# Two couples of heads weighed directly behind each other, into the two halves of one PSUM bank, with five buffers of turned weights

## The chip, the cores and the metric

The kernel runs on one core of a Trainium2 chip. The metric is the device time of one execution in microseconds (us), the median of several runs. A core has five engines that work through their own queues in order: TensorE (PE in the profile, its weight loads PEld), VectorE (DVE), ScalarE (ACT), GpSimd (POOL) and SyncE (SP, which here only issues DMAs). They wait for each other through semaphores.

## The reference

A trunk of two decoder layers over 256 positions of width 2048, in float32. Every layer is `x <- LN(alpha*x + mixer(x))` and then `x <- LN(alpha*x + sqrelu_mlp(x))`. The mixer of layer 0 has sliding-window attention A (16 query heads, 2 key heads, sinks) and dilated attention B (8 heads, three patterns that are merged by their softmax denominators). The mixer of layer 1 has stick-breaking attention C (16 heads, no softmax) and latent attention D (16 heads). The part that the change touches is, in each of them, the last line of this:

```
s = einsum('bqhd,bshd->bhqs', q, k) * scale      # scores
p = softmax(where(valid, s + bias, -inf))        # or the stick-breaking weights
o = einsum('bhqs,bshd->bqhd', p, v)              # the values are weighed
y = concat(heads of both groups);  out = einsum('bse,ed->bsd', y, w_out)
```

## The kernel before, in words

All weights come from memory as units of 128 x 1024 float32. `Stream._split` makes a high part (`w_hi`, ScalarE, L120) and a low part (`w_lo`, VectorE, L121) of each, and every projection is three products: high by high, low by high, high by low. `ws` (L329, L332) writes features to partitions, `as_` (L379 to L381) positions. Both work unit by unit, and between two units they call `pump`, which does one step of attention (`attn_step`). So attention is woven into the projections: the projections keep TensorE busy while ScalarE and VectorE work on the weights of attention.

Attention runs in jobs: A (16 heads), B0 and B1 (4 heads with 3 patterns each), C0, D0, C1, D1 (8 heads each). A step takes a couple of heads, and on TensorE writes its scores (`qk`, L708, tiles `sc`). VectorE and ScalarE then make weights `S` of them in the following steps. A flip (`flip`, L260) transposes the weights of one head on TensorE into the tile `pt`, and ScalarE copies that to `pT` (L262); each step does at most one flip. Two steps behind the flip of a couple's second head comes the weighing (`weigh`): four matmuls (L279 and L281) of 64 output columns of the array, the even head into partitions 0 to 63 and the odd head into 64 to 127 of the tile `o`, which has 256 columns of float32 and one buffer, a PSUM bank. The two heads' fp32 matmuls show as 4 instructions for each of the two lines. With the last pattern of a couple, `o` is evicted: ScalarE casts it to the high part of `y` (L285), and VectorE makes the low part of `o` and the high part (L286). In B1, C1 and D1 the tiles that take the place of `y` are named `x`.

Within one step the order on the queues is: the weighing, the flip, the stages of VectorE and ScalarE, then the scores of the next couple (the number behind `at_step`'s step is that order). What `pump` calls first are small functions that were put off (`late`), among them the rotation of D's queries (`rotate`, L982 to L984, on VectorE). `pT` has four buffers, `S` four.

Of the kernel before, what the change touches and what calls it, by code (L numbers as in the profile page):

```python
# [11 lines left out]
F32 = mybir.dt.float32  # L12
F32R = mybir.dt.float32r
BF16 = mybir.dt.bfloat16
# [4 lines left out]
P = 128  # L19
S = 256  # L20
# [143 lines left out]
class Trunk:  # L164
    def __init__(self, tc, ctx, args):
        self.tc = tc
        self.nc = tc.nc
        self.a = args
        self.split_ahead = 3
        self.dma_ahead = 5  # L170
        pool = lambda name, bufs, **kw: ctx.enter_context(tc.tile_pool(name=name, bufs=bufs, **kw))
        self.const = pool("const", 1)
        self.raw = pool("raw", 6)
        self.spl = pool("spl", 4)
        self.res = pool("res", 1)
        self.small = pool("small", 5)
        self.ps = pool("ps", 1, space=bass.MemoryType.PSUM)
        self.w = Stream(self)
        self.side = deque()
        self.late = deque()  # L180
        self.todo = deque()
        self.due = {}
        self.flips = deque()
        self.s_live = 0
        self.i = 0
        self.turn = 0
# [26 lines left out]
    def attn_step(self):  # L213
        i = self.i
        self.i += 1
        if self.flips and self.flips[0][0] <= i:
            _, job, h, u = self.flips.popleft()
            self.at_step(i, 2, self.flip, job, h, u)
            if h % 2:
                self.at_step(i + 2, 1, self.weigh, job, (h - 1, h), u)  # L220
        for _, _, fn, args in sorted(self.due.pop(i, []), key=lambda t: t[:2]):
            fn(*args)
        if not self.todo or i < self.turn:
            return
        job, h, u = self.todo[0]
        per, pair = job.per, (h, h + 1)
        if h not in job.s:
            need = 2 if per > 1 else 1
            if self.s_live + need > self.s_bufs:
                return  # L230
            self.s_live += need
            if per > 1:
                for g in pair:
                    job.s[g] = self.at.tile([P, per * 384], F32, name="S", bufs=self.s_bufs)
            else:
                both = self.at.tile([P, 768], F32, name="S", bufs=self.s_bufs)
                job.s[h], job.s[h + 1] = both[:, 0:384], both[:, 384:768]
        self.todo.popleft()
        self.turn = i + job.pace
        scs = [self.ps.tile([P, 384], F32, name="sc", bufs=2) for _ in pair]  # L240
        self.qk(scs, [job.score(g, u) for g in pair])
        for j, (g, sc) in enumerate(zip(pair, scs)):
            job.stages[0](g, u, sc, job.s[g])
            if u == per - 1:
                for n, fn in enumerate(job.stages[1:]):
                    self.at_step(i + j + 1 + n, 3, fn, g, job.s[g])
        if u == per - 1:
            self.flips.extend((i + j + job.lag, job, g, v) for v in range(per) for j, g in enumerate(pair))
# [5 lines left out]
    def flip(self, job, h, u):  # L254
# [9 lines left out]
        if u == job.per - 1 and (job.per > 1 or h % 2):  # L264
            self.s_live -= 1

    def weigh(self, job, heads, u):
        nc = self.nc
        first, last = u == 0, u == job.per - 1
        if first and heads[0] % 2 == 0:  # L270
            job.o = self.ps.tile([P, S], F32, name="o")
        o = job.o
        for blk in range(2):
            for h in heads:
                rows = slice((h % 2) * HD, (h % 2) * HD + HD)
                w = job.pt[(h, u)]
                v = job.value(h, u, blk)
                if blk == 0:
                    nc.tensor.matmul(o[rows, :], v, w[:, 0:S], start=first, stop=False, skip_group_check=True)  # L279
                else:  # L280
                    nc.tensor.matmul(o[rows, P:S], v, w[:, S:S + P], start=False, stop=last, skip_group_check=True)  # L281
        if last and heads[-1] % 2:
            y = job.y(len(job.out))
            yh, yl, _ = y
            nc.scalar.copy(yh, o)  # L285
            nc.vector.tensor_tensor(yl, o, yh.bitcast(F32), op=ALU.subtract)  # L286
            job.out.append(y)
            job.left -= 1
# [155 lines left out]
    def setup(self):  # L444
        nc, a, const = self.nc, self.a, self.const
        self.x = self.res.tile([P, 2, D], F32, name="x_res")
        xv = a["x"][0].rearrange("(t p) d -> p t d", p=P)
        cuts = (0, 256, 512, 1024, 1536, 2048)
        for c0, c1 in zip(cuts[:1], cuts[1:]):
            nc.scalar.dma_start(self.x[:, :, c0:c1], xv[:, :, c0:c1])  # L450
        nc.scalar.preload_act_table_set("natural_log_exp_and_others")
        zeros = self.at.tile([P, 512], BF16, name="zeros")
        nc.vector.memset(zeros, 0.0)
        self.keep_clock(IDLE[0], zeros)
        self.ident = const.tile([P, P], F32, name="ident")
        nc.sync.dma_start(self.ident, a["ident"])
        self.w._dma(1)
        for c0, c1, ahead in zip(cuts[1:], cuts[2:], (2, 4, 5, 6)):
            nc.sync.dma_start(self.x[:, :, c0:c1], xv[:, :, c0:c1])
            self.w._dma(ahead)  # L460
        gb = self.at.tile([16, 8, P], F32, name="gb")
        rg = self.at.tile([6, P], F32, name="rg")
        self.sinks = const.tile([P, 16], F32, name="sinks")
        self.masks = self.at.tile([P, 4, 384], F32, name="masks")
        small = [(gb[:, i * 2:i * 2 + 2, :], a[nm].rearrange("l (k p) -> k l p", p=P))
                 for i, nm in enumerate(("ln1_g", "ln1_b", "ln2_g", "ln2_b"))]
        small += [(rg[0:4, :], a["odd_q_norm_g"][0].rearrange("(k p) -> k p", p=P)),
                  (rg[4:6, :], a["odd_kv_norm_g"][0].rearrange("(k p) -> k p", p=P)),
                  (self.masks, a["m_even"]), (self.sinks, a["even_sinks"][0].unsqueeze(0).to_broadcast([P, 16]))]

        def load(some):
            for dst, src in some:
                nc.gpsimd.dma_start(dst, src)

        def gate():

            nc.gpsimd.tensor_copy(self.masks[:, 0, 0:1], self.xT[10][0][:, 0:1].bitcast(F32))

        self.late.extend([lambda: None] * 6)
        self.late.append(gate)  # L480
        self.late.extend(lambda some=small[i:i + 2]: load(some) for i in range(0, 8, 2))
        self.mhalf = const.tile([P, 2], F32, name="mhalf")
        nc.vector.memset(self.mhalf, -0.5)
        self.xT = LazyTiles(self.transposed(None))
        self.gbc = const.tile([P, 134], F32, name="gbc")
        self.side.append(self.gains(gb, rg))
# [380 lines left out]
    def odd(self):  # L867
        nc = self.nc
        self.masks = self.at.tile([P, 2, 384], F32, name="masks")
        self.rope_f = self.at.tile([P, S], F32, name="rope_f")  # L870
        self.rope_t = self.at.tile([P, 2, 64], F32, name="rope_t")
        for t, nm in ((self.rope_t, "rope_t"), (self.rope_f, "rope_f"), (self.masks, "m_odd")):
            self.late.append(lambda t=t, nm=nm: nc.gpsimd.dma_start(t, self.a[nm]))
        cq = self.as_(self.xT, KT, 512)
        zq = self.rms(cq, 512)
        self.pump()
        ck = self.as_(self.xT, KT, 288)
        kr = self.at.tile([P, 2, 96], F32, name="kr", bufs=1)
        nc.gpsimd.memset(kr[:, :, 0:64], 0.0)
        kt_ = self.at.tile([P, 2, 32], F32, name="krt", bufs=1)  # L880
        ks = self.at.tile([P, 2, 32], F32, name="krs", bufs=1)
        for t in range(2):
            rt = self.rope_t[:, t, :]
            nc.vector.tensor_copy(ks[:, t, 0:16], ck[t][:, 272:288])
# [255 lines left out]
    def go(self):  # L1140
        tc = self.tc
        self.plan()
        for layer in range(2):
            if layer == 0:
                self.s_bufs, self.pt_bufs, self.qk_bufs, self.y_bufs = 4, 4, {"qk": 15}, 10
            else:
                self.s_bufs, self.pt_bufs, self.qk_bufs, self.y_bufs = 4, 4, {"c": 8, "d": 10}, 14
            with tc.tile_pool(name=f"at{layer}", bufs=1) as self.at:
                if layer == 0:
                    self.setup()  # L1150
                last, st = self.even() if layer == 0 else self.odd()
                assert not self.side and not self.todo
            self.layer_norm(last, st, 1, layer)
            with tc.tile_pool(name=f"mp{layer}", bufs=1) as self.mp:
                last, st = self.mlp(layer)
                if layer == 1:
                    self.final(last, st)
            if layer == 0:
                self.layer_norm(last, st, 2, layer)
# [33 lines left out]
```

## Time and profile before

| | us |
|---|---|
| median of 3 runs | 2181.27 (2180.08 to 2182.53) |
| the profiled execution | 2179.61 |
| its span in the trace | 2177.8 |
| PE busy | 2160.6 (99%) |
| DVE busy | 1393.6 (64%) |
| ACT busy | 1064.2 (49%) |

Busy time is the union of an engine's instructions in the trace; the ends of matmuls are modelled, so for TensorE the start of one instruction to the start of the next is the better measure. A row of the timeline merges equal instructions that follow each other. In square brackets stands how long the engine was idle before the row, and what released it; "issue" is time in which it waited for nothing that the profile shows.

### The profile page before, as it was taken

What the parts mean: (1) busy time and instruction counts of PE and PEld (TensorE: products, weight loads), DVE (VectorE), ACT (ScalarE), POOL (GpSimd) and SP (SyncE); (2) the same over time, 40 slices, a digit from 0 to 9 for tenths busy, and PEclk for the clock granted to TensorE, in tenths of its full rate; (3) what the DMA queues carried; (4) which work ended last, traced back from release to release, by engine and by line L of the source; (5) the groups of instructions that cost most, each with busy time, mean ns of one, the idle gap of its engine ahead of it and who ended that gap; (6) DMA issues with size and microseconds to landing.
All of it is one profiled execution on the core that took longest, in us unless ns stands there. A gap on an engine that the chain in (4) does not pass through costs nothing.

```text
span 2177.8 us, 29447 instructions
## 1 busy us (share of the span) xinstructions
PE 2160.6 (99%) x11323; PEld 1816.3 (83%) x11324; DVE 1393.6 (64%) x1912; ACT 1064.2 (49%) x1532; POOL 35.3 (2%) x65
## 2 busy tenths in 40 slices
PE   9999999999999999999999999999999999999998
PEld 8878887888888888888888887778888888888886
DVE  5765566775465556456568888878645655554656
ACT  4554444554354345355345667545534534543542
POOL 0000000000000000000012000000000000000000
PEclk9999999999999999999999999999999999999999
DMA  8446554665656665656558544466565656556553
GB/s 278 148 134 182 157 164 148 197 197 195 192 184 199 191 190 193 193 176 202 191 151 212 170 143 149 153 196 209 202 193 175 203 194 192 184 197 190 185 200 118
DMA packets 222269, 399.02 MB, mean 183 GB/s; under 512 B 12778, under 2 KB 52416, under 8 KB 221360
## 3 DMA queue, kind: packets, MB, share of 16 engines
q1 hardware_dynamic: 219152, 386.51, 56.3%
q0 software_dynamic: 2416, 9.84, 2.0%
q8 instruction: 88, 1.44, 0.3%
q10 hardware_dynamic: 560, 0.79, 0.1%
q14 instruction: 53, 0.43, 0.1%
HBM read 395.00 MB, written 2.10 MB: 182 GB/s over the span
## 4 chain that ended last, share of the span: by engine, by line
PE 94%; issue 2%; DVE 1%; DMA 1%; ACT 1%; POOL 1%; POOLq 0%; SPq 0%; ACTq 0%; DVEq 0%
PE acc L332 18%; PE acc L379 15%; PE acc L380 15%; PE acc L381 15%; PE acc L329 9%; PE sc L332 5%; PE sc L329 3%; PE pt L332 3%; PE o L332 3%; PE sc L708 2%; PE o L329 1%; PE pt L329 1%; PE pt L260 1%; PE o L279 1%; DVE w_lo L121 1%
## 5 line engine op out<-in xcount | busy, mean ns | idle before, releaser
L121 DVE TENSOR_TENSOR w_lo<-raw,w_hi 128x1024 fp32r<-128x1024 f32 (+3 forms) x748 | 883.9, 1198 | 601.7 <-ACT w_hi L120 597.7
L120 ACT CAST w_hi<-raw 128x1024 fp32r<-128x1024 f32 (+3 forms) x748 | 760.1, 1030 | 729.7 <-PE acc L381 439.8
L332 PE MATMUL acc<-x,w_hi 128*128 128x512 f32 x1824 | 453.8, 394 | 2.7 <-DVE x L529 2.5
L379 PE MATMUL acc<-w_hi,h_hi 128*128 128x512 f32 x1016 | 395.3, 389 | 0.0
L380 PE MATMUL acc<-w_lo,h_hi 128*128 128x512 f32 x1016 | 395.3, 389 | 0.0
L381 PE MATMUL acc<-w_hi,h_lo 128*128 128x512 f32 x1016 | 395.2, 389 | 0.0
L332 PEld LDWEIGHTS acc<-x,w_hi 128*128 128x128 f32 x1824 | 331.2, 189 | 66.6 <-ACT w_hi L120 2.5
L329 PEld LDWEIGHTS acc<-x,w_lo 128*128 128x128 f32 x1824 | 243.2, 190 | 17.8 <-issue 3.8
L329 PE MATMUL acc<-x,w_lo 128*128 128x256 f32 x1824 | 253.8, 284 | 0.0
L381 PEld LDWEIGHTS acc<-w_hi,h_lo 128*128 128x128 f32 x1016 | 190.7, 188 | 39.6
L379 PEld LDWEIGHTS acc<-w_hi,h_hi 128*128 128x128 f32 x1016 | 190.8, 188 | 39.4
L380 PEld LDWEIGHTS acc<-w_lo,h_hi 128*128 128x128 f32 x1016 | 190.8, 188 | 39.2
L332 PE MATMUL sc<-x,w_hi 128*128 128x512 f32 x512 | 138.7, 392 | 0.0
L379 PE MATMUL acc<-w_hi,x 128*128 128x512 f32 (+1 forms) x304 | 119.5, 393 | 0.3 <-DVE x L528 0.2
L381 PE MATMUL acc<-w_hi,x 128*128 128x512 f32 (+1 forms) x304 | 115.8, 381 | 0.0
L380 PE MATMUL acc<-w_lo,x 128*128 128x512 f32 (+1 forms) x304 | 115.7, 381 | 0.0
L345 ACT ACTIVATE xfull<-acc 128x256 f32<-128x256 f32 x130 | 49.7, 384 | 127.7 <-PE acc L332 77.5
L332 PEld LDWEIGHTS sc<-x,w_hi 128*128 128x128 f32 x512 | 91.1, 189 | 14.6
L329 PE MATMUL sc<-x,w_lo 128*128 128x256 f32 x512 | 84.3, 282 | 0.0
L329 PEld LDWEIGHTS sc<-x,w_lo 128*128 128x128 f32 x512 | 76.6, 190 | 6.4
L332 PE MATMUL pt<-x,w_hi 128*128 128x512 f32 x256 | 79.3, 391 | 0.0
L332 PE MATMUL o<-x,w_hi 128*128 128x512 f32 x256 | 78.9, 389 | 0.0
(209 smaller groups left out, 1956.4 us busy)
## 6 DMA issues: line engine op xcount, KB each, us to landing
raw<-in_mlp_w SPq DMA_DIRECT2D x512, 512.0 KB, 3.9
raw<-in_even_w_in SPq DMA_DIRECT2D x92, 512.0 KB, 4.1
raw<-in_odd_w_in SPq DMA_DIRECT2D x56, 512.0 KB, 4.5
raw<-in_odd_w_out SPq DMA_DIRECT2D x32, 512.0 KB, 3.6
raw<-in_even_w_out SPq DMA_DIRECT2D x24, 512.0 KB, 3.9
gb_rows<-in_ln_g POOLq DMA_DIRECT2D x3, 1024.0 KB, 5.0
gb_rows<-in_ln_b POOLq DMA_DIRECT2D x3, 1024.0 KB, 7.1
raw<-in_odd_w_uq SPq DMA_DIRECT2D x8, 384.0 KB, 4.7
```

The source lines that it names most:

```text
L120: nc.scalar.copy(h, r)
L121: nc.vector.tensor_tensor(l, r, h.bitcast(F32), op=ALU.subtract)
L260: nc.tensor.transpose(pt[:, b * P:(b + 1) * P], st[:, u * 384 + b * P:u * 384 + (b + 1) * P], self.ident)
L279: nc.tensor.matmul(o[rows, :], v, w[:, 0:S], start=first, stop=False, skip_group_check=True)
L329: nc.tensor.matmul(banks[f][:, S:2 * S], lo[:, c:c + P], xs[kt + kk][0], start=False, stop=wide and kt + kk == nkt - 1, skip_group_check=True)
L332: nc.tensor.matmul(banks[f], hi[:, c:c + P], xs[kt + kk][2], start=kt + kk == 0, stop=not wide and kt + kk == nkt - 1, skip_group_check=True)
L345: nc.scalar.activation(t, bank[:, S:2 * S], AF.Copy, scale=scale)
L379: nc.tensor.matmul(outs[t], xh[:, ts], hi[:, c:c + width], start=first, stop=False, skip_group_check=True)
L380: nc.tensor.matmul(outs[t], xh[:, ts], lo[:, c:c + width], start=False, stop=False, skip_group_check=True)
L381: nc.tensor.matmul(outs[t], xl[:, ts], hi[:, c:c + width], start=False, stop=last, skip_group_check=True)
L708: nc.tensor.matmul(sc[:, cols], q[:, qs], k[:, ks], start=True, stop=True, skip_group_check=True)
```

## The change

`weigh_two` now stands where `weigh` was called. It keeps the arguments of a weighing until there are two, and then does both. The tile `o` is 512 columns wide, a whole bank, and the couples take its halves in turn. Since the turned weights of a couple are held until the next couple's are there, `pT` gets a fifth buffer. To make room for it, small tiles that are needed early (`zeros`, the gains `gb` and `rg`, the rotary table `rope_t` and three tiles of the shared rotary key) are put into buffers of `pT` and `S`.

```diff
@@ -181,6 +181,8 @@
         self.flips = deque()
+        self.pend = []
+        self.o_half = 0
         self.s_live = 0
@@ -217,7 +219,7 @@
             if h % 2:
-                self.at_step(i + 2, 1, self.weigh, job, (h - 1, h), u)
+                self.at_step(i + 2, 1, self.weigh_two, job, (h - 1, h), u)
@@ -264,11 +266,22 @@
+    def weigh_two(self, *args):
+
+        self.pend.append(args)
+        if len(self.pend) == 2:
+            for a in self.pend:
+                self.weigh(*a)
+            self.pend = []
+
     def weigh(self, job, heads, u):
         nc = self.nc
         first, last = u == 0, u == job.per - 1
-        if first and heads[0] % 2 == 0:
-            job.o = self.ps.tile([P, S], F32, name="o")
+        if first:
+            if self.o_half == 0:
+                self.o_bank = self.ps.tile([P, 2 * S], F32, name="o")
+            job.o = self.o_bank[:, self.o_half * S:(self.o_half + 1) * S]
+            self.o_half = 1 - self.o_half
         o = job.o
@@ -449,7 +462,7 @@
-        zeros = self.at.tile([P, 512], BF16, name="zeros")
+        zeros = self.at.tile([P, 512], BF16, name="pT", bufs=self.pt_bufs)
@@ -458,8 +471,8 @@
-        gb = self.at.tile([16, 8, P], F32, name="gb")
-        rg = self.at.tile([6, P], F32, name="rg")
+        gains = self.at.tile([16, 9, P], F32, name="S", bufs=self.s_bufs)
+        gb, rg = gains[:, 0:8, :], gains[0:6, 8, :]
@@ -868,17 +881,15 @@
-        self.rope_t = self.at.tile([P, 2, 64], F32, name="rope_t")
+        early = self.at.tile([P, 2, 224], F32, name="S", bufs=self.s_bufs)
+        self.rope_t, kr, kt_, ks = (early[:, :, a:b] for a, b in ((0, 64), (64, 160), (160, 192), (192, 224)))
...
-        kr = self.at.tile([P, 2, 96], F32, name="kr", bufs=1)
         nc.gpsimd.memset(kr[:, :, 0:64], 0.0)
-        kt_ = self.at.tile([P, 2, 32], F32, name="krt", bufs=1)
-        ks = self.at.tile([P, 2, 32], F32, name="krs", bufs=1)
@@ -1142,9 +1153,9 @@
-                self.s_bufs, self.pt_bufs, self.qk_bufs, self.y_bufs = 4, 4, {"qk": 15}, 10
+                self.s_bufs, self.pt_bufs, self.qk_bufs, self.y_bufs = 4, 5, {"qk": 15}, 10
             else:
-                self.s_bufs, self.pt_bufs, self.qk_bufs, self.y_bufs = 4, 4, {"c": 8, "d": 10}, 14
+                self.s_bufs, self.pt_bufs, self.qk_bufs, self.y_bufs = 4, 5, {"c": 8, "d": 10}, 14
```

What this makes of the queues is seen best in the order of the instructions. A row is the line, the operation, what it writes and reads (buffer numbers of tiles left out), the size of what it writes, and the semaphores that it waits for: DVE_49 counts what VectorE has done, Activation_49 what ScalarE has done. The lines of the changed kernel are 13 higher here (L279 is L292, L281 is L294, L286 is L299, L260 is L262).

This is TensorE's queue before, where the first couple of job A is weighed, in a step between two units of the projection (`acc`):

```order
L381 MATMUL acc<-w_hi,x_126 128x512
L279 MATMUL o<-pT,qk 64x256 x2
L281 MATMUL o<-pT,qk 64x128 x2
L260 MATMUL pt<-ident,S 128x128 [waits DVE_49,Activation_49]
L260 MATMUL pt<-ident,S 128x128 [waits DVE_49]
L260 MATMUL pt<-ident,S 128x128
L708 MATMUL sc<-qk 128x128 [waits DVE_49] x2
L708 MATMUL sc<-qk 128x256 x2
```

Two steps further on in the same queue, before, the second couple is weighed:

```order
L381 MATMUL acc<-w_hi,x_181 128x512
L279 MATMUL o<-pT,qk 64x256 [waits DVE_49]
L279 MATMUL o<-pT,qk 64x256
L281 MATMUL o<-pT,qk 64x128 x2
L260 MATMUL pt<-ident,S 128x128 [waits Activation_49]
L260 MATMUL pt<-ident,S 128x128 x2
L708 MATMUL sc<-qk 128x128 [waits DVE_49] x2
L708 MATMUL sc<-qk 128x256 x2
```

And this is TensorE's queue in the changed kernel at this second place:

```order
L394 MATMUL acc<-w_hi,x_180 128x512
L292 MATMUL o<-pT,qk 64x256 x2
L294 MATMUL o<-pT,qk 64x128 x2
L292 MATMUL o<-pT,qk 64x256 [waits DVE_49]
L292 MATMUL o<-pT,qk 64x256
L294 MATMUL o<-pT,qk 64x128 x2
L262 MATMUL pt<-ident,S 128x128 [waits Activation_49]
L262 MATMUL pt<-ident,S 128x128 x2
L721 MATMUL sc<-qk 128x128 x2
L721 MATMUL sc<-qk 128x256 x2
```

The first weighing has moved from the first place to the second, and the wait for VectorE stands between the two weighings.

VectorE's queue before, where the second couple of D0 is evicted, behind a rotation of queries (`d`, `rope_f`):

```order
L346 SCALAR_TENSOR_TENSOR d<-acc,xfull 128x256 [waits Activation_49] x4
L982 TENSOR_TENSOR rtmp<-d,rope_f 32x512 [waits DVE_49]
L983 TENSOR_TENSOR d<-d,rope_f 32x512
L984 TENSOR_TENSOR d<-d,rtmp 32x512 [waits DVE_49]
L286 TENSOR_TENSOR y<-o,y 128x256 [waits Activation_49]
```

The same place of VectorE's queue in the changed kernel:

```order
L359 SCALAR_TENSOR_TENSOR d<-acc,xfull 128x256 [waits Activation_49] x4
L993 TENSOR_TENSOR rtmp<-d,rope_f 32x512 [waits DVE_49]
L994 TENSOR_TENSOR d<-d,rope_f 32x512
L995 TENSOR_TENSOR d<-d,rtmp 32x512 [waits DVE_49]
L299 TENSOR_TENSOR y<-o,y 128x256 [waits Activation_49] x2
```

Both couples' low parts now stand behind the rotation; the second weighing on TensorE stands between them.

## Rows read from the trace of the kernel before

**Rows 1.** The page: the span, and TensorE's busy time.

```profile
span 2177.8 us, 29447 instructions
PE 2160.6 (99%) x11323; PEld 1816.3 (83%) x11324; DVE 1393.6 (64%) x1912; ACT 1064.2 (49%) x1532; POOL 35.3 (2%) x65
```

**Rows 2.** Windows: length, busy us (instructions) of PE, PEld, DVE, ACT, POOL; clock, DMA.

```profile
90.00:160.00 70.00, 70.00 (x423) 54.62 (x422) 52.47 (x132) 42.60 (x112) 0.00 (x0) 1.00 0.48 140
1235.00:1435.00 200.00, 199.72 (x1108) 160.48 (x1107) 162.27 (x310) 128.71 (x265) 0.00 (x0) 1.00 0.47 148
```

**Rows 3.** Timeline (start, us, engine, line): couple 1 of A is weighed.

```profile
99.20 0.39 PE L381 MATMUL acc<-w_hi,x 128*128 128x512 f32 x1
...
99.52 0.20 PEld L279 LDWEIGHTS o<-pT,qk 128*64 128x64 f32 x4 [0.35 <-issue]
99.52 0.65 PE L279 MATMUL o<-pT,qk 128*64 128x256 f32 x4
...
100.00 0.39 PE L281 MATMUL o<-pT,qk 128*64 128x128 f32 x4
...
100.32 0.55 PE L260 MATMUL pt<-ident,S 128*128 128x128 f32 x3
...
100.80 0.93 PE L708 MATMUL sc<-qk 64*128 64x128 f32 x8
```

**Rows 4.** Timeline of TensorE: two flips with no weighing ahead of them.

```profile
92.18 0.49 PE L260 MATMUL pt<-ident,S 128*128 128x128 f32 x3
92.60 0.93 PE L708 MATMUL sc<-qk 64*128 64x128 f32 x8
...
104.29 0.39 PE L381 MATMUL acc<-w_hi,x 128*128 128x512 f32 x1
104.52 0.49 PE L260 MATMUL pt<-ident,S 128*128 128x128 f32 x3
```

**Rows 5.** Timeline: behind the weighing of couple 2 of A.

```profile
108.52 0.55 PE L260 MATMUL pt<-ident,S 128*128 128x128 f32 x3
108.64 0.37 ACT L285 CAST y<-o 128x256 fp32r<-128x256 f32 x1 [1.05 <-PE o L281]
...
109.04 0.42 DVE L286 TENSOR_TENSOR y<-o,y 128x256 fp32r<-128x256 f32 x1 [0.20 <-ACT y L285]
```

**Rows 6.** Timeline: behind the weighing of couple 4 of D1.

```profile
1430.51 0.50 PE L379 MATMUL acc<-w_hi,x 128*128 128x512 f32 x1
...
1431.04 0.42 DVE L286 TENSOR_TENSOR x<-o,x 128x256 fp32r<-128x256 f32 x1 [0.43 <-ACT x L285]
```

**Rows 7.** Timeline: a flip at the end of B1 waits for ScalarE.

```profile
358.78 0.48 ACT L262 COPY pT<-pt 128x384 f32<-128x384 f32 x1 [2.63 <-PE pt L260]
...
359.31 0.55 PE L260 MATMUL pt<-ident,S 128*128 128x128 f32 x3 [0.62 <-ACT pT L262]
```

**Rows 8.** Timeline: ScalarE and VectorE behind the weighing at 252.43 (B0).

```profile
253.88 0.48 ACT L262 COPY pT<-pt 128x384 f32<-128x384 f32 x1 [2.65 <-PE pt L260]
...
255.34 1.23 DVE L121 TENSOR_TENSOR w_lo<-raw,w_hi 128x1024 fp32r<-128x1024 f32 x1 [2.85 <-ACT w_hi L120]
```

**Rows 9.** Timeline: behind the weighing of couple 2 of D0.

```profile
1310.48 0.55 PE L260 MATMUL pt<-ident,S 128*128 128x128 f32 x3
...
1312.06 0.68 DVE L984 TENSOR_TENSOR d<-d,rtmp 32x512 f32<-32x512 f32 x1
...
1312.76 0.42 DVE L286 TENSOR_TENSOR y<-o,y 128x256 fp32r<-128x256 f32 x1
```

**Rows 10.** Timeline: behind the weighing of couple 2 of C1.

```profile
1368.57 1.58 PE L708 MATMUL sc<-d 96*128 96x128 f32 x8
...
1370.20 0.42 DVE L286 TENSOR_TENSOR x<-o,x 128x256 fp32r<-128x256 f32 x1
```

**Rows 11.** The page's groups: the low parts of the split weights (us, mean ns).

```profile
L121 DVE TENSOR_TENSOR w_lo<-raw,w_hi 128x1024 fp32r<-128x1024 f32 (+3 forms) x748 | 883.9, 1198 | 601.7 <-ACT w_hi L120 597.7
```

**Rows 12.** Timeline: TensorE just before the end of the program.

```profile
2170.76 1.12 PE L692 MATMUL pt<-x_res,g_row 128*128 128x512 f32 x2 [1.77 <-ACT g_row L684]
```

## The prediction

> **What bounds the kernel now.** I read the page first, then the stretches in which attention runs, then the timeline around single weighings. TensorE is busy for 2160.6 us of a span of 2177.8 us [rows 1]. In the attention stretches it is busy without a gap (70.00 of 70.00 us and 199.72 of 200.00 us), at a granted clock of 1.00, while VectorE is busy for 52.47 of 70 us and 162.27 of 200 us [rows 2]. So TensorE's queue is the path. It works in order, and whatever stops it for 1 us makes the program 1 us longer: no wait elsewhere on it in these stretches could take the loss up. ScalarE and VectorE have slack, but each works its queue in order too, and what matters is how soon they reach one particular instruction.
>
> **What the change does to TensorE's queue.** There are 36 weighings: 8 of job A, 12 of jobs B0 and B1 (2 couples of heads by 3 patterns, each), 8 of C and 8 of D. They become 18 pairs. Nothing is computed more or less often: the same matmuls, the same 28 evictions (L285 and L286). What is new is that the first weighing of a pair is moved to the step of the second, and that they share a bank.
>
> *What is saved.* A weighing standing alone in a step costs an entry and an exit. Before it, the last matmul of the projection takes from 99.20 to 99.52, so 0.32 us until the weighing starts [rows 3]; before a flip the same kind of matmul takes from 104.29 to 104.52, so 0.23 us [rows 4]. Behind it, the flip takes from 100.32 to 100.80, so 0.48 us to the scores [rows 3]; a flip that stands behind the projection takes from 92.18 to 92.60, so 0.42 us [rows 4]. One removed entry and exit is worth 0.09 + 0.06 = 0.15 us, and 18 times that is 2.7 us. The upper bound is the whole 0.35 us that the weight loads stand still ahead of a weighing [rows 3], 18 x 0.35 = 6.3 us; the lower is nothing. I take 2.7, since start-to-start times of matmuls are what the path is made of. The weighing itself (0.80 us, from 99.52 to 100.32 [rows 3]) is moved, not saved.
>
> *What is added.* In the new order the second weighing's first matmul waits for VectorE, and the first weighing's does not. The instruction behind that wait is found by counting the increments of the semaphore in the built program: the first couple's low part (L286 before, L299 now), which stands between the two weighings. The new bank is one tile, and its second half is not written until the first half has been read out. Before, the same kind of wait was for the eviction of the previous couple, a step or more earlier, and cost nothing. Now TensorE, ScalarE and VectorE must hand the work on: last matmul, copy of the high part, low part, and only then the next weighing. Behind the waiting matmul on TensorE stand the flip, the scores and the whole next unit of the projection, so all of them are late.
>
> How long this takes stands in the trace of before, because the second couple's own eviction stands at just that place of both queues. For couple 2 of A, TensorE went on at 108.52; ScalarE's copy began at 108.64 and VectorE's low part ran from 109.04 for 0.42 us, to 109.46 [rows 5]. From ScalarE's end to TensorE's start a release takes 0.05 us: the copy that began at 358.78 ended at 359.26 and the flip began at 359.31 [rows 7]. I take the same for VectorE's. So the second weighing can start at 109.51 and not at 108.52: 0.99 us. The same reading for the last pair (couples 3 and 4 of D1) is 1431.04 + 0.42 + 0.05 - 1430.51 = 1.00 us [rows 6], and eight other pairs lie between these two in size. In the two pairs of B that hold an eviction (pattern 3 of one couple, pattern 1 of the next) nothing is evicted at that place before; there ScalarE had been idle for 2.65 us and VectorE was idle for 2.85 us [rows 8], so I take 0.99 there as well. Twelve pairs: 12 x 0.99 = 11.9 us.
>
> Two pairs are worse, since VectorE has other work ahead of the low part. In couple 2 of D0 three rotary operations stand first, the last of them 0.68 us long; the low part starts at 1312.76, so the stall is 1312.76 + 0.42 + 0.05 - 1310.48 = 2.75 us [rows 9]. In couple 2 of C1 it starts at 1370.20 and TensorE went on at 1368.57, which makes 2.10 us [rows 10]. In the other four of the 18 pairs (two in each of B0 and B1) no eviction stands between, and no wait: they only save.
>
> Sum: 11.9 + 2.75 + 2.10 - 2.7 = +14.0 us. The two long terms lie between 0.99 each (if VectorE, which no longer evicts the couple before, has cleared its queue in time) and what was read.
>
> *Edits that I cost at nothing.* The fifth buffer of turned weights: with two couples held back, a fifth flip would otherwise wait; with it none of the flips' copies waits for anything but the weighings ahead of it in the same step, and the flip itself is behind these on TensorE anyway. The shared buffers ("zeros" in pT, the gains and the early rotary tables in S): their last readers are done before the first score is written there, and their loads keep their places in GpSimd's queue with the same waits. If a cover of these were gone, it would be one wait of about the 0.05 to 1 us above, not fourteen. ScalarE and VectorE do their evictions two at a time; the second copy follows the second weighing as it did before, so the flip's copy behind it is not later against TensorE.
>
> **The rivals.**
>
> *The halves don't hold each other up* (the other side). If the second weighing could start while the first half is read out, only the saving would be left: 2181.27 - 2.7 = 2178.6, or 2175.0 with the 6.3 us of the upper bound. It decides where the stall is under 2.7 / 14 = 0.19 us for each pair. For it speaks that the two halves are different columns, each with readers of its own. Against it speaks the new program order, where the wait stands, and that even the low part alone takes 0.42 us [rows 5]. The Trainium skill, "PSUM — Partial Sum Buffer", section "PSUM bank collisions raise a hardware error", says that two engines may not touch one bank in the same partitions at once, whichever columns they use, and that waits are to be set by bank; by that rule the sum is the +14.0, by a rule that goes by columns it is the -2.7. No row of before shows a half of a bank read while the other is written. Chance 7 in 100.
>
> *VectorE's queue is longer at these places than it was.* The low part of a split unit takes 1.198 us [rows 11]. TensorE comes to the second couple's step a little earlier against the others than before, since the first weighing is gone from the step ahead. If one such instruction slips in front of the low part in 7 of the 12 short pairs, that is 8.4 us more (2203.7); in all 12, 14.4 us more (2209.7). Against it: the cast and the split ahead of the low part hang on the flip one step earlier, which moves together with TensorE. Chance of above 2205: 10 in 100.
>
> *The clock falls.* TensorE is idle 14 times for about 1 us, twice for over 2 us. If it then ran the stretch behind (4.0 us from the flip at 104.52 to the flip at 108.52 [rows 4, 5]) at the lower level, each would add 4 us and all 56: 2251. Against it: the engine was idle for 1.77 us before the last matmuls [rows 12] and the clock is 1.00 in the stretches read. Chance 3 in 100.
>
> **How the numbers follow.** The profiled execution took 2179.61 us, 1.81 us more than its span and 1.7 us under the median of 2181.27 us; adding 14.0 to the median gives 2195.3 us. The likeliest case has 80 in 100. Its low end: both long stalls at 0.99 (2.9 us less) and the saving at 6.3 (3.6 us less), so +7.5, less 1.3 us for the spread of the runs: 2187.5. Its high end: 7 queued splits, +22.4, and 1.3 us of spread: 2205. About 0.2% (4.4 us) is what a measurement of this kernel can tell. Slower has 0.93 (0.80 + 0.10 + 0.03). The 0.07 of the first rival divides into 0.04 within 0.2% and 0.03 faster (a saving near the upper bound).
>
> **What would show it.** In the profile after: idle time of TensorE of some 16 us in total ahead of the weighing's first matmuls, released by VectorE's low part, in 14 places, 12 of them near 0.9 us, in D0 and C1 one each above 2 us; TensorE's busy time hardly changed; four pairs of weighings without a gap. ScalarE's idle time ahead of the high parts stays, and VectorE's ahead of the second low part of a pair grows, since it waits for the second weighing. I would be wrong if the weighings of a pair started within 1 us of each other everywhere, if a stall of this size were taken up because TensorE later waits less for weights, or if the long stalls appeared in most pairs.

## The result, and the profile after

| | before | changed |
|---|---|---|
| median (lowest to highest), us | 2180.61 (2180.08 to 2182.53), 6 runs | 2197.23 (2195.03 to 2202.22), 6 runs |
| profiled execution, us | 2179.61 | 2197.77 |
| its span, us | 2177.8 | 2196.0 |
| ratio of the times | | 1.0077, 95% interval 1.0067 to 1.0087 |

The changed kernel is slower by 16.6 us between the medians, and by 18.2 us between the two profiled executions. The forecast was +14.0 us, and its range, 2187.5 to 2205.0, holds the median.

The head of the page of the changed kernel (its lines answer to [rows 1]) shows that TensorE does not work longer, although the span has grown:

```profile
span 2196.0 us, 29434 instructions
PE 2159.0 (98%) x11323; PEld 1817.3 (83%) x11324; DVE 1394.5 (64%) x1912; ACT 1064.2 (48%) x1532; POOL 35.5 (2%) x65
```

It is busy for 1.6 us less than before, so nearly all of the loss is time in which it stands still. Where, its waits of the changed kernel say (engine and line, what was waited for, us in total, times, longest us):

```profile
PE sc L529 <- DVE x_res L626: 4.1, 6, 0.9
...
PE o L292 <- DVE y L299: 10.4, 9, 2.7
...
PE o L292 <- DVE x L299: 6.3, 5, 2.5
...
PE sc L529 <- DMA x_res<-in_x: 2.5, 2, 1.6
PE acc L1005 <- DVE c L359: 1.6, 1, 1.6
```

Two of these rows are new. The weighing (L292) waits 14 times for the low part (L299), 16.7 us in all. Eleven of the waits are 0.93 us, one in A is 1.22, one in D0 is 2.70 and one in C1 is 2.54. The other rows were there before with less: 3.9 and 0.8 us for `x_res`, 0.7 us for `c`.

The timeline of the changed kernel at couples 3 and 4 of A shows one short wait whole (start in us, us, engine, line, operation, and in brackets the idle time before it and what ended it):

```profile
124.78 0.65 PE L292 MATMUL o<-pT,qk 128*64 128x256 f32 x4
...
125.27 0.39 PE L294 MATMUL o<-pT,qk 128*64 128x128 f32 x4
...
125.70 0.37 ACT L298 CAST y<-o 128x256 fp32r<-128x256 f32 x1 [1.10 <-PE o L294]
...
126.11 0.42 DVE L299 TENSOR_TENSOR y<-o,y 128x256 fp32r<-128x256 f32 x1 [0.25 <-ACT y L298]
...
126.59 0.65 PE L292 MATMUL o<-pT,qk 128*64 128x256 f32 x4 [0.93 <-DVE y L299]
...
127.07 0.39 PE L294 MATMUL o<-pT,qk 128*64 128x128 f32 x4
```

Read it as a relay. The first weighing begins at 124.78 and, at 0.80 us for one, would make room at 125.58. ScalarE begins its copy at 125.70, VectorE its low part at 126.11 and ends it at 126.53, and at 126.59 the second weighing begins. That is 126.59 - 125.58 = 1.01 us of standstill from start to start; the idle time of 0.93 in the bracket is a little shorter, since it counts from the modelled end of the last matmul.

In B0 the changed kernel has a pair with no eviction between, and its timeline shows the second weighing close behind the first:

```profile
241.32 0.65 PE L292 MATMUL o<-pT,qk 128*64 128x256 f32 x4
...
241.80 0.39 PE L294 MATMUL o<-pT,qk 128*64 128x128 f32 x4
...
242.02 0.60 PE L292 MATMUL o<-pT,qk 128*64 128x256 f32 x4
...
242.77 0.55 PE L262 MATMUL pt<-ident,S 128*128 128x128 f32 x3
```

From 241.32 to 242.02 is 0.70 us and from there to the flip 0.75, where a weighing before took 0.80 to the flip [rows 3].

The two long waits of the changed kernel, on VectorE and TensorE, answer to [rows 9] and [rows 10]:

```profile
1319.85 0.42 DVE L299 TENSOR_TENSOR y<-o,y 128x256 fp32r<-128x256 f32 x1
...
1320.33 0.65 PE L292 MATMUL o<-pT,d 128*64 128x256 f32 x4 [2.70 <-DVE y L299]
...
1380.29 1.22 DVE L121 TENSOR_TENSOR w_lo<-raw,w_hi 128x1024 fp32r<-128x1024 f32 x1
...
1381.42 0.42 DVE L299 TENSOR_TENSOR x<-o,x 128x256 fp32r<-128x256 f32 x1
...
1381.89 0.65 PE L292 MATMUL o<-pT,c 128*64 128x256 f32 x4 [2.54 <-DVE x L299]
```

In D0 the low part stands behind the rotary operations, as in [rows 9]. In C1 it stands behind a whole split of weights, 1.22 us. That split was there before too, just ahead of the low part of [rows 10], as the timeline of the kernel before shows:

```profile
1369.07 1.22 DVE L121 TENSOR_TENSOR w_lo<-raw,w_hi 128x1024 fp32r<-128x1024 f32 x1
```

What has changed is when it comes: 1.30 us behind the start of the weighing before (1367.77 to 1369.07), 1.81 us behind the start of the pair's first weighing now (1378.48 to 1380.29). VectorE's queue has fallen back by 0.51 us against TensorE's.

The windows of the changed kernel (us, busy time of PE, PEld, DVE, ACT and POOL with counts, granted clock of TensorE, share of the DMA engines, GB/s) show what followed these two waits:

```profile
1320.00:1324.00 4.00, 3.67 (x22) 2.92 (x23) 1.32 (x5) 2.65 (x8) 0.00 (x0) 1.00 0.04 10
...
1382.00:1386.00 4.00, 4.00 (x19) 3.13 (x20) 2.21 (x6) 1.73 (x3) 0.00 (x0) 0.68 0.36 131
1386.00:1390.00 4.00, 4.00 (x19) 3.21 (x18) 3.30 (x7) 0.99 (x4) 0.00 (x0) 0.89 0.20 62
```

Behind D0's wait the clock stayed at 1.00. Behind C1's it fell: part of both windows ran at the lower level (1.2 instead of 2.4 GHz). The matmuls show it too. In the timeline of the same kernel two neighbours of the projection begin 0.43 us apart, and 0.23 us apart once the clock is back:

```profile
1385.61 0.63 PE L394 MATMUL acc<-w_hi,y 128*128 128x512 f32 x1
...
1386.04 0.63 PE L392 MATMUL acc<-w_hi,y 128*128 128x512 f32 x1
...
1387.57 0.39 PE L394 MATMUL acc<-w_hi,y 128*128 128x512 f32 x1
...
1387.80 0.39 PE L392 MATMUL acc<-w_hi,y 128*128 128x512 f32 x1
```

From the scores behind this weighing (1382.70) to the next flip (1388.48) it took 5.78 us; before, the same stretch took 4.16 us, from 1368.57 to 1372.73. The lower clock cost 1.6 us there.

### The profile page after: what moved, and what is told of

It reads as the page before. It is cut to its first block, busy times and chain, and to the rows that moved or that the text cites. A ratio compares the mean times of both kernels' runs of the same rounds, so it can differ in the third digit from the quotient of the medians.

```text
span 2196.0 us, 29434 instructions
## 1 busy us (share of the span) xinstructions
PE 2159.0 (98%) x11323; PEld 1817.3 (83%) x11324; DVE 1394.5 (64%) x1912; ACT 1064.2 (48%) x1532; POOL 35.5 (2%) x65
## 4 chain that ended last, share of the span: by engine, by line
PE 92%; DVE 3%; issue 2%; DMA 1%; ACT 1%; POOL 1%; POOLq 0%; SPq 0%; ACTq 0%; DVEq 0%
PE acc L345 18%; PE acc L392 14%; PE acc L393 14%; PE acc L394 14%; PE acc L342 9%; PE sc L345 5%; PE sc L342 3%; PE pt L345 3%; PE o L345 3%; PE sc L721 1%; PE o L342 1%; PE pt L342 1%; PE pt L262 1%; DVE w_lo L121 1%; PE o L292 1%
## 5 line engine op out<-in xcount | busy, mean ns | idle before, releaser
L342 PEld LDWEIGHTS acc<-x,w_lo 128*128 128x128 f32 x1824 | 243.3, 190 | 17.8 <-issue 3.5
```

Source lines behind the costliest of these rows:

```text
L342: nc.tensor.matmul(banks[f][:, S:2 * S], lo[:, c:c + P], xs[kt + kk][0], start=False, stop=wide and kt + kk == nkt - 1, skip_group_check=True)
```

## The experiments

**Theory.** The second weighing waits because the program reads the first half of the bank (ScalarE's copy, VectorE's low part) between the two writes. **Rivals:** the loss comes with the shared bank itself, the fifth buffer or the moved small tiles; or a slower eviction costs time anywhere, through VectorE's load, and not through the wait. The first four kernels ran on one chip, with a median of 2180.45 us for the kernel before (33 runs), the other four on another, with 2180.91 us (15 runs).

**Both weighings first, then both evictions.** Nothing else of the change is touched: the same banks, buffers and tiles.

```diff
         if len(self.pend) == 2:
-            for a in self.pend:
-                self.weigh(*a)
+            ends = [self.weigh(*a) for a in self.pend]
+            for end in ends:
+                end()
             self.pend = []
...
-        if last and heads[-1] % 2:
+
+        def end():
+            if not (last and heads[-1] % 2):
+                return
             y = job.y(len(job.out))
             yh, yl, _ = y
             nc.scalar.copy(yh, o)
...
+        return end
+
```

> The matmuls of both couples stand first, and both evictions behind them; nothing else differs from the changed kernel. Theory (TensorE stands still while the first half is read out, 14 times): the 16.7 us of standstill are gone, and what is left is the saving, 18 times 0.15 us and some 0.10 us more for each pair that follows without a gap: 4.5 us under the kernel before, about 2176 us. Rival (bunching two evictions, holding two couples back, and moving the weighings out of their steps is what costs): it stays near 2197 us, as the work is bunched as before.

Measured: 2177.88 us (2177.01 to 2178.38, 11 runs), ratio 0.9986 (0.9977 to 0.9995). This is under both kernels. Its timeline at the same pair of A:

```profile
123.04 0.65 PE L293 MATMUL o<-pT,qk 128*64 128x256 f32 x4
...
123.52 0.39 PE L295 MATMUL o<-pT,qk 128*64 128x128 f32 x4
...
123.74 0.60 PE L293 MATMUL o<-pT,qk 128*64 128x256 f32 x4
...
124.61 0.37 ACT L302 CAST y<-o 128x256 fp32r<-128x256 f32 x1 [1.75 <-PE o L295]
...
125.01 0.42 DVE L303 TENSOR_TENSOR y<-o,y 128x256 fp32r<-128x256 f32 x1 [0.90 <-ACT y L302]
125.47 0.37 ACT L302 CAST y<-o 128x256 fp32r<-128x256 f32 x1 [0.49 <-DVE y L303]
```

The second weighing begins 0.70 us behind the first, and both evictions follow the second weighing. No wait at a weighing is left. The order of the readers alone takes back all of the loss. One hand-over between the halves remains: ScalarE's copy of the second half waits 0.49 us for VectorE's low part of the first, but it stands behind TensorE's writes, where no weighing of the pair waits for it.

Of the 18 x 0.25 = 4.5 us that were expected under the time before, 2.6 came. In layer 0 the pairs give even more, 0.31 us each: TensorE's lead over the kernel before grows from 0.74 us (106.98 against 107.72) to 3.21 us (354.13 against 357.34) over eight pairs. What is missing was lost behind that. The waits of this kernel on TensorE show some of it:

```profile
PE pt L262 <- ACT pT L264: 1.7, 3, 0.8
PE sc L535 <- DMA x_res<-in_x: 1.5, 2, 1.2
PE acc L1011 <- DVE c L365: 1.3, 1, 1.3
```

The same waits were 0.6, 0.8 and 0.7 us before, so 2.4 us more together. Of the first, two flips at the end of B1 wait 0.57 and 0.78 us, as they do in the changed kernel; the third, 0.37 us at 1321.99, comes behind a cast of weights on ScalarE, not behind an eviction. The other two rows also vary where no pairs are made (below). What the rest of the 4.5 us went to was not tried by itself.

**One couple at a time.** Only the number is changed at which the held weighings are done, so that every couple is weighed in its own step again, into halves of a bank, with all the rest of the change in place.

```diff
-        if len(self.pend) == 2:
+        if len(self.pend) == 1:
```

> Each couple is weighed in its own step again, but into the halves of one bank in turn, with five buffers of pT and the small tiles where the change put them. Theory: no eviction stands between two weighings, the wait for the half before is long over, so the time is that of the kernel before, within 0.2%. Rival (the shared bank by itself, the moved tiles or the fifth buffer cost something, as the late start and a longer wait in the projection of D's queries in the profile after could be read): 1 to 3 us over the kernel before.

Measured: 2180.62 us (2180.15 to 2183.65, 11 runs), ratio 1.0002 (0.9993 to 1.0011). No wait of L292 is left. The shared bank, the fifth buffer and the moved tiles cost nothing that can be measured by themselves: 0.2 us between the medians, at most 2.4 us by the interval. The rival falls as a source of the 16.6 us. In this kernel TensorE waits 1.8 us for `c` (0.7 us before) at no loss that can be measured, so this wait is not the pairs' doing.

**Pairs in layer 0 alone** (A, B0 and B1: 10 pairs, 6 of them with an eviction between).

```diff
-        if len(self.pend) == 2:
+        if len(self.pend) == self.couples:
...
             if layer == 0:
+                self.couples = 2
...
             else:
+                self.couples = 1
```

> Pairs in layer 0 (A, B0, B1), one couple at a time in layer 1. Theory: 6 standstills of about 1.0 us, 10 pairs that save 0.15 us and 4 of them 0.10 us more: +4.4 us, about 2185 us, and no fall of the clock. Rival (each pair costs the same, whatever stands between): 10 of 18 parts of 16.6 us, +9.2 us, about 2190 us. Rival (the two long standstills and the clock make up nearly all): within 2 us of the kernel before.

Measured: 2185.18 us (2184.88 to 2186.74, 11 runs), ratio 1.0022 (1.0013 to 1.003). L292 waits 6 times, 5.9 us in all:

```profile
PE o L292 <- DVE y L299: 5.0, 5, 1.2
...
PE o L292 <- DVE x L299: 0.9, 1, 0.9
```

By the readings above the sum is 5 x 1.01 + 1.29 for the stalls (1.29 is that of the wait of 1.22 in A), less 10 x 0.15 and 4 x 0.15 (a pair without a gap takes 1.45 us in place of 1.60): +4.2 us. Measured are +4.7. The terms hold for a part of the program, and layer 1 with its two long waits has the larger share.

**ScalarE alone reads the bank.** The copy goes to a small tile in SBUF, and VectorE makes both parts from there, which gives it one more operation for each eviction and takes one off the relay.

```diff
-            nc.scalar.copy(yh, o)
-            nc.vector.tensor_tensor(yl, o, yh.bitcast(F32), op=ALU.subtract)
+            of = self.small.tile([P, 2, S], F32, name="xfull", bufs=2)[:, 0, :]
+            nc.scalar.copy(of, o)
+            nc.vector.tensor_copy(yh, of)
+            nc.vector.tensor_tensor(yl, of, yh.bitcast(F32), op=ALU.subtract)
```

> The changed kernel, but ScalarE alone reads the bank, into a float32 tile of SBUF, and VectorE makes both parts from that. Theory: the standstill is the time to the last reader of the first half: 0.12 us to ScalarE's start, 0.37 us of copy, 0.05 us of release, 0.54 us in all 14 places, the two long ones too, since VectorE's queue no longer counts: 7.6 us less the saving of 3.1 us, +4.5 us, about 2185 us. Rival (VectorE's queue is what is overloaded): VectorE does 28 operations more, so it is no faster than the changed kernel, 2197 us or over.

Measured: 2185.62 us (2184.89 to 2187.86, 11 runs), ratio 1.0025 (1.0016 to 1.0033), although VectorE does more. Its waits on TensorE:

```profile
PE o L292 <- ACT xfull L299: 6.8, 14, 0.5
```

and its timeline at the pair of D0, where the changed kernel stood still for 2.70 us:

```profile
1312.92 0.37 ACT L299 COPY xfull<-o 128x256 f32<-128x256 f32 x1 [0.20 <-PE o L294]
1313.21 0.69 DVE L995 TENSOR_TENSOR rtmp<-d,rope_f 32x512 f32<-32x512 f32 x1
1313.35 0.65 PE L292 MATMUL o<-pT,d 128*64 128x256 f32 x4 [0.47 <-ACT xfull L299]
```

The wait ends with the copy while VectorE is only beginning its rotary operations. All 14 waits are now between 0.47 and 0.53 us, the long ones too: it was VectorE's queue that made the long ones long, and the number of reads in the relay that set the rest.

**The low part twice**, in the changed kernel and, as a control, in the kernel before. The line is only repeated, with the same output.

```diff
             nc.vector.tensor_tensor(yl, o, yh.bitcast(F32), op=ALU.subtract)
+            nc.vector.tensor_tensor(yl, o, yh.bitcast(F32), op=ALU.subtract)
```

> The changed kernel with VectorE's low part of every eviction done twice (the same values again), 28 more operations of 0.42 us. Theory: 14 of them stand between two weighings and lengthen the standstill by 0.42 to 0.44 us each: 5.9 to 6.2 us over the changed kernel, about 2203 us; the other 14 are hidden. Rival (VectorE's load as a whole sets the time): 28 times 0.42, 11.8 us more, about 2209 us. Rival (the wait is only for ScalarE's copy): no more than the changed kernel.

> The kernel before with the low part done twice, the control of the run above. Theory: nobody waits for it there, so no change, within 0.2% of 2180.5 us. Rival (VectorE's load as a whole): 11.8 us more, 2192 us.

Measured: 2207.16 us (2204.82 to 2207.27, 4 runs), ratio 1.012 (1.0104 to 1.0135), for the changed kernel; 2181.10 us (2180.19 to 2182.57, 11 runs), ratio 1.0001 (0.9992 to 1.001), for the kernel before. The same 28 added operations cost nothing where nobody waits for the bank. The waits of the changed kernel with the low part twice:

```profile
PE o L292 <- DVE y L300: 14.6, 9, 3.2
...
PE o L292 <- DVE x L300: 8.6, 5, 3.0
```

Each of the 14 waits has grown by 0.46 to 0.51 us, 6.5 us in all, as far as the theory goes. The profiled execution (2204.82 us) is 7.0 us above that of the changed kernel; the other three are above 2207, at a mean granted clock of 0.996 to 0.997 where the profiled one has 0.998. Its windows around the end of the wait of 3.16 us in D0 (1324.02) and behind it show a lower clock there:

```profile
1320.00:1324.00 4.00, 0.86 (x9) 0.47 (x8) 3.71 (x7) 0.85 (x3) 0.00 (x0) 0.87 0.68 236
...
1322.00:1326.00 4.00, 1.98 (x11) 1.27 (x12) 1.86 (x4) 0.37 (x1) 0.00 (x0) 0.62 0.23 81
1326.00:1330.00 4.00, 4.00 (x12) 3.19 (x12) 2.70 (x7) 3.25 (x7) 0.00 (x0) 0.52 0.02 4
```

Behind C1's wait of 3.05 us it stayed at 1.00 in the same execution. So the clock is the likely source of the 4 us beyond what was expected, but the three longer executions left no trace, and of them this is argued and not shown.

**C1 without pairs**, to see whether the fall of the clock belongs to C1.

```diff
-        if len(self.pend) == 2:
+        if len(self.pend) == (1 if args[0].name == "C1" else 2):
```

> The changed kernel, but in job C1 one couple is weighed at a time; the other 16 pairs stay. Theory: C1's two standstills go (2.6 and 1.0 us) and 0.3 us of saving with them, and the stretch at a lower clock that stood behind the long one (1.6 us): 4.9 us less than the changed kernel, about 2192.3 us, and the granted clock stays at 1.00 behind D0's standstill of 2.7 us as it did. If the low clock does not belong to C1's standstill, 3.3 us less, about 2193.9 us, and a low stretch somewhere else. Rival (each pair costs the same): 2 of 18 parts of 16.6 us, 1.8 us less, 2195.4 us.

Measured: 2194.27 us (2192.46 to 2195.82, 5 runs), ratio 1.0059 (1.0047 to 1.0072). Twelve waits of 13.2 us are left, D0's 2.70 among them, and now the window behind that one has the lower clock:

```profile
1320.00:1324.00 4.00, 3.68 (x15) 2.66 (x16) 1.31 (x5) 1.68 (x7) 0.00 (x0) 0.57 0.01 3
```

The time agrees with what C1's two stalls are worth without the clock (2193.9), but the spread of the runs holds the other two expectations as well. What the profile adds is that the fall is not C1's.

**The changed kernel once more**, for a second trace.

> The changed kernel once more, for a second profile. Theory: 14 standstills of the same lengths, 16.7 us in sum. Whether the stretch at the lower clock behind C1's long standstill comes again is open: if it does, it belongs to that place; if not, it comes and goes, and the spread of the runs (2195.0 to 2202.2 us) is that.

Measured: 2197.01 us. The 14 waits are the same to 0.01 us. The windows behind the long waits have changed places:

```profile
1320.00:1324.00 4.00, 4.00 (x18) 3.12 (x15) 1.20 (x5) 2.85 (x8) 0.00 (x0) 0.57 0.01 4
...
1382.00:1386.00 4.00, 3.18 (x21) 2.60 (x22) 2.35 (x6) 1.73 (x3) 0.00 (x0) 1.00 0.47 156
```

Here the clock fell behind D0's wait and stayed at 1.00 behind C1's, the reverse of the first trace. The waits belong to the program; the fall of the clock comes and goes from one execution to the next.

## Why the prediction was right

**The standstill.** The step was that TensorE waits in 14 of the 18 pairs for the first couple's low part. It does, in just these places. The short stall was put at 0.99 us from the second couple's own eviction; eleven measure 1.01. The twelfth, couple 2 of A, is 1.29. In the kernel before, VectorE has a split there:

```profile
107.62 1.23 DVE L121 TENSOR_TENSOR w_lo<-raw,w_hi 128x1024 fp32r<-128x1024 f32 x1
```

In the changed kernel it has the same split, and the low part behind it:

```profile
107.72 1.22 DVE L121 TENSOR_TENSOR w_lo<-raw,w_hi 128x1024 fp32r<-128x1024 f32 x1
108.85 0.41 DVE L299 TENSOR_TENSOR y<-o,y 128x256 fp32r<-128x256 f32 x1
```

Before, the weighing began at 107.72, 0.10 us behind the split, and VectorE was free again when the copy ended. In the changed kernel the first weighing began at 107.23, 0.49 us ahead of the split: the copy was done at 108.52, and the low part had to wait until 108.85.

**The two long ones.** D0 was put at 2.75 and measures 2.77. C1 was put at 2.10 and measures 2.61, 0.51 more, by which VectorE's split and low part come later against TensorE than before. The forecast took VectorE's lateness over from the trace of before; that the two queues shift against each other it had only as a rival, not in the sum. All stalls together are 11 x 1.01 + 1.29 + 2.77 + 2.61 = 17.8 us, where the forecast had 11.9 + 2.75 + 2.10 = 16.75.

**The saving.** One removed entry and exit was put at 0.15 us. Couples 4 and 6 of A show it: what TensorE lags behind its time before grows from 0.66 us (124.12 against 124.78) to 1.52 us (140.60 against 142.12), so by 0.86 for one more pair, and 1.01 - 0.86 is 0.15. What the forecast left out is that two weighings directly behind each other also take 0.15 us less (0.70 + 0.75 for 2 x 0.80), in the four pairs without a wait. That makes 2.7 + 0.6 us.

**The sum.** 17.8 - 2.7 - 0.6 = 14.5 us, for the 14.0 forecast. The mechanism was right; that the sum came so close is partly luck, since 1.0 us of standstill too little and 0.6 us of saving too little nearly cancel. Of the 18.2 us between the two profiled executions 3.7 are left. The lower clock behind C1 is 1.6 of them, which the forecast had only as a rival. The first `x_res` comes later from its DMA, so that the work begins about 0.5 us later (the clock fell once there as well, see the last section), and the wait for `c` is 0.9 us longer; both waits differ in the same way in kernels that were not slower. Some 0.3 us, by an estimate from the starts there, were lost at the end of B1; a flip waits there 0.78 us for ScalarE's copy (365.61) that had a weighing ahead of it before. The last 0.4 lies between the two attention stretches and was not followed up. The two profiled executions are also not alike: the one of before lies 1.0 us under its median, the one of the changed kernel 0.5 us over its own.

**The rivals.** *The halves don't hold each other up* falls for this program order: the wait is there, and it follows the readers, 0.47 to 0.53 us with one, 0.93 with two, 1.39 with three where VectorE's queue is clear. The Trainium skill, "PSUM — Partial Sum Buffer", section "PSUM bank collisions raise a hardware error", wants waits set by bank. By that rule the second half is not to be written while the first is read, and the traces agree: no eviction of a half overlaps a weighing into the same bank (wait of 0.93 us); what the chip would do without the wait no run here shows. The rival's time, 2178.6 by the saving alone, was nearly reached (2177.88), but by moving the readers behind both writes. *VectorE's queue is longer* came true in part: in two pairs, one of A and one of C1, TensorE came earlier against VectorE, as the rival says, and the stall was 0.3 and 0.5 us longer. But the split that held the low part up was ahead of it before too, no new one slipped in, and it was two pairs and not 7. *The clock falls* came true in part: not behind the waits of 0.93 us, but behind one of the two long ones in each trace of the changed kernel, at 1.6 us where it was measured and not at 4 us for each of 14.

## What to carry to other kernels

When two results go into halves of one bank, write both before anything reads either: here the order of the program alone decided whether TensorE stood still between them (2197.23 against 2177.88 us). Whether two banks in place of the two halves would take the wait away as well was not run. A wait that a change creates can be priced ahead from the trace of before, by the relay that already stands at that place (last matmul, copy, low part, release), if one also looks at what else the reader's queue has there: that made 2.77 out of 1.01 us in D0. How far the change shifts the two queues against each other belongs to it, which the sum here left out: 0.5 us in C1. And take as many readers off the relay as can read a copy instead: one engine that reads the bank instead of two cut 14 waits from 16.7 to 6.8 us.

## What the runs showed of the hardware

Around a standstill of 2.5 us or more TensorE's granted clock went to its lower level in some executions and not in others, with the same waits to 0.01 us: behind 2.54 in one trace of the changed kernel, behind 2.70 in the other and behind 2.70 in the kernel without pairs in C1, at 3.16 and not at 3.05 in one trace with the low part twice. In this last one it fell while the engine still stood: the clock is 0.87 from 1320 to 1324 us, and the weighing goes on at 1324.02. None of the waits of 0.93 us was followed by it.

It is not the pairs' alone, and it also came with shorter waits. The first trace of the changed kernel has it at the start of the program, behind a wait for `x_res`, ahead of the first weighing:

```profile
7.53 0.83 PE L529 MATMUL sc<-ident,x_res 128*128 128x128 f32 x4 [1.55 <-DMA x_res<-in_x]
...
8.00:12.00 4.00, 4.00 (x15) 3.27 (x14) 3.30 (x4) 2.05 (x3) 0.00 (x0) 0.59 1.02 384
```

In the kernel before with the low part twice the clock is 0.92 from 1200 to 1204 us and 0.65 in the 4 us behind, around a wait of 1.76 us for `c`, and 1.00 around about the same wait in the changed kernel. What decides between one execution and the next stays open.
